# Hybrid decoder layer on one core: strips of the row sums issued together, and the late gathered tiles summed on TensorE

## The chip, the core and the metric

One core of a Trainium2 chip runs the whole layer in one launch. Its engines are TensorE (PE in the profile; its weight loads are PEld), VectorE (DVE), ScalarE (ACT), GpSimd (POOL) and SyncE (SP), each with its own instruction queue, and 16 DMA engines that they share. The metric is the device time of one launch in microseconds; the times are medians over several runs on one chip, and a profile is one execution. Lower is better.

## The reference

One decoder layer on 1024 tokens of 1024 features, in float32. The first half is a mixture of mLSTM heads and dilated attention with an output projection; the second half, where the change lies, is a retrieval of single-neuron experts:

```python
def peer(h, w_query, sub_keys1, sub_keys2, expert_u, expert_v):
    ...
    v1, i1 = lax.top_k(s1, PEER_TOPK)
    v2, i2 = lax.top_k(s2, PEER_TOPK)
    cand = (v1[..., :, None] + v2[..., None, :]).reshape(T, PEER_HEADS, PEER_TOPK * PEER_TOPK)
    vc, ic = lax.top_k(cand, PEER_TOPK)
    ...
    idx = (e1 * N_KEYS + e2).reshape(T, PEER_HEADS * PEER_TOPK)
    gate = jax.nn.softmax(vc, axis=-1).reshape(T, PEER_HEADS * PEER_TOPK)

    def block(args):
        xb, ib, gb = args
        u = expert_u[ib]
        pre = jnp.einsum('td,tkd->tk', xb, u).astype(jnp.float32)
        a = jax.nn.gelu(pre, approximate=False) * gb
        return jnp.einsum('tk,tkd->td', a, expert_v[ib])
```

Each token picks 8 heads x 16 = 128 of 16384 experts; the dot products of its row with 128 rows of `expert_u` give 128 coefficients, and the sum of 128 rows of `expert_v` by these coefficients is added to the token's row `x2`.

## The kernel before

The 1024 tokens are eight tiles of 128, in three groups: tiles 0 and 1, tiles 2 to 5, tiles 6 and 7 (`GROUPS`). Each group passes the projections, attention and mLSTM, the output projection and the queries (`queries`, with `top16` on DVE), and then `pick` makes expert numbers and gates.

The experts are computed in two ways. Group 1 (tiles 2 to 5) is dense: `spread_gates` writes a full table of gates (16384 experts x 512 tokens) through TensorE (L737), ACT and POOL, and `dense_experts` multiplies the tokens with all of `expert_u` (tile pu) and the coefficients with all of `expert_v` (tile pv). Each of these products is three full-width float32r matmuls (L153 to L155) from a high and a low half of both operands; ACT makes the high halves of the tables (L756, L788), DVE the low ones (L758, L790), with two buffers each.

Groups 0 and 2 (tiles 0, 1, 6, 7) are gathered. `experts_in` (U) fetches for each of the 128 picks one row of `expert_u` per token by an indirect DMA issued from POOL (`gather`, L801, 512 KB, five buffers `gt`), and DVE forms the dot product (L813). The sum over `expert_v` (V) has two forms:

- `experts_out`, for the tiles that are not in `ON_PE` (6 and 7): one gather for each pick, and one DVE instruction that multiplies the rows by the coefficient of each token and adds them up (L855).
- `experts_out_pe`, for the tiles in `ON_PE` (0 and 1): here a gather fetches the 128 rows of one token, so the picks lie on the partitions and TensorE sums over them. The coefficients are transposed first (L825), and `pick` has transposed the indices (L700 to L704, tile idxt). The loop runs over two blocks of 64 tokens and 32 steps. A step takes a pair of tokens, 32 apart: DVE builds their weights (L836, tile wv, four buffers), 128 x 32 each, of which one column holds the token's coefficients and the others are zero. Two tokens times two halves of 512 features are four matmuls (L843), each with a 128 x 32 weight and a strip of 32 partitions of the accumulator `po` as target: strips 0 and 2 (q = 0, 2) read the first row buffer of the pair, strips 1 and 3 the second.

The order of the V and U steps is written out at the end: U0 U1 V0 V1 U6 V6 U7 V7. They are traced after all the other work, `dense_experts` too, but the program is ordered by a scheduler that simulates the engines: an instruction takes the first place on its engine at which its operands are ready in the simulation, the earlier in the trace first; within `tc.high_priority()` a matmul goes ahead of whatever else is ready. The order on each engine is then fixed, and on the chip each engine works through it in that order, waiting for semaphores. So the gathered work of tiles 0 and 1 lies beside the attention, the queries and the spreading of group 2 and 1, and that of tiles 6 and 7 beside the dense experts.

Of the kernel before, what the change touches and what calls it, by code (L numbers as in the profile page):

```python
# [11 lines left out]
F32 = mybir.dt.float32  # L12
F32R = mybir.dt.float32r
I32 = mybir.dt.int32
# [6 lines left out]
P = 128  # L21
# [3 lines left out]
NT = T // P  # L25
GROUPS = ((0, 2), (2, 4), (6, 2))
DENSE = 1
ON_PE = (0, 1)
HT = 2
HW = HT * P  # L30
EG = 8
# [3 lines left out]
AH = 8  # L35
# [8 lines left out]
def hybrid_layer(ctx, tc, x, g1, w_in, w_if, conv_w, conv_b, wq, wk, if_b, mh_g, skip, qn_g, kn_g,  # L44
                 rel_bias, onehot, w_out, g2, w_query, keys, expert_u, expert_ut, expert_v, out, dbg=None):
    nc = tc.nc
# [4 lines left out]
    sp = ctx.enter_context(tc.tile_pool(name="sparse", bufs=1))  # L51
# [144 lines left out]
    IDX, IDXT, GATE = {}, {}, {}  # L196
# [442 lines left out]
    def pick(rt, g, t, gr, h0=0, h1=AH):  # L639

        dense = g == DENSE
        H = h1 - h0
        ix = INDS[t][:, :, h0:h1]
        vc, ic = (a[:, h0:h1] for a in BEST[t])

        sh = rt.tile([P, H, 16], U32, name="sh")
        nc.vector.tensor_scalar(sh, ic, 4, 7, op0=ALU.logical_shift_right, op1=ALU.bitwise_xor)
        nc.vector.tensor_scalar(ic, ic, 16, 31, op0=ALU.bitwise_or, op1=ALU.bitwise_and)
        nc.vector.tensor_scalar(ic, ic, 2, None, op0=ALU.logical_shift_left)
        ab = rt.tile([P, 2, H, 16], U32, name="abi")  # L650
        nc.vector.tensor_tensor(ab[:, 0], ic, sh, op=ALU.logical_shift_right)
        nc.vector.tensor_tensor(sh, ab[:, 0], sh, op=ALU.logical_shift_left)
        nc.vector.tensor_tensor(ic, ic, sh, op=ALU.bitwise_xor)
        nc.vector.tensor_scalar(ab[:, 1], ic, 2, 15, op0=ALU.logical_shift_right, op1=ALU.bitwise_and)
        abf = rt.tile([P, 2, H, 16], BF16, name="abf")
        nc.vector.tensor_copy(abf, ab)
        ixf = rt.tile([P, 2, H, 16], BF16, name="ixf")
        nc.vector.tensor_copy(ixf, ix)
        if h0 == 0:
            EF[t] = rt.tile([P, 3, AH, 16], F32, name="ef", bufs=1 if dense else 2)  # L660
            if not dense:
                GATE[t] = sp.tile([P, AH, 16], F32, name="gate", bufs=4)
                IDX[t] = sp.tile([P, P], I32, name="idx", bufs=4)
        ef = EF[t][:, :, h0:h1]
        full = [P, H, 16, 16]
        for s in range(2):
            of = rt.tile(full, BF16, name="of")
            nc.scalar.copy(of, ixf[:, s, :, :, None].to_broadcast(full))
            one = rt.tile(full, BF16, name="one")
            nc.vector.tensor_tensor(one, abf[:, s, :, None, :].to_broadcast(full),  # L670
                                    rank16[:, None].to_broadcast(full), op=ALU.is_equal)
            nc.vector.tensor_tensor(one, one, of, op=ALU.mult)
            for n in (8, 4, 2):
                nc.vector.tensor_tensor(one[:, :, 0:n], one[:, :, 0:n], one[:, :, n:2 * n], op=ALU.add)
            nc.vector.tensor_tensor(ef[:, s], one[:, :, 0], one[:, :, 1], op=ALU.add)
        if not dense:
            e1, e2 = (ef[:, k].rearrange("p h k -> p (h k)") for k in range(2))
            nc.vector.scalar_tensor_tensor(IDX[t][:, h0 * 16:h1 * 16], e1, 128.0, e2, op0=ALU.mult, op1=ALU.add)
        ex = ef[:, 2]
        nc.vector.tensor_tensor(ex, vc, vc[:, :, 0:1].to_broadcast([P, H, 16]), op=ALU.subtract)  # L680
        nc.scalar.activation(ex, ex, AF.Exp)
        sm = rt.tile([P, H], F32, name="smx")
        nc.vector.tensor_reduce(sm, ex, AX.X, ALU.add)
        nc.vector.reciprocal(sm, sm)
        if dense:
            nc.vector.tensor_tensor(ex, ex, sm[:, :, None].to_broadcast([P, H, 16]), op=ALU.mult)
            pe = pst.tile([P, 3, P], F32, name="pe", tag="tp")
            for s in range(3):
                nc.tensor.transpose(pe[:, s], ef[:, s].rearrange("p h k -> p (h k)"), ident)
            ids = gr.tile([P, 2, P], BF16, name="ids", bufs=GROUPS[DENSE][1])  # L690
            nc.scalar.copy(ids, pe[:, 0:2])
            gate = gr.tile([P, P], F32, name="grow", bufs=GROUPS[DENSE][1])
            nc.scalar.copy(gate, pe[:, 2])
            ROWS[t] = ids, gate
        else:
            nc.vector.tensor_tensor(GATE[t][:, h0:h1], ex, sm[:, :, None].to_broadcast([P, H, 16]), op=ALU.mult)
            if t in ON_PE and h1 == AH:
                pe = pst.tile([P, 2, P], F32, name="pei", tag="tp")
                for k in range(2):
                    nc.tensor.transpose(pe[:, k], EF[t][:, k].rearrange("p h k -> p (h k)"), ident)  # L700
                eT = rt.tile([P, P], F32, name="eT")
                nc.scalar.copy(eT, pe[:, 1])
                IDXT[t] = sp.tile([P, P], I32, name="idxt", bufs=len(ON_PE))
                nc.vector.scalar_tensor_tensor(IDXT[t], pe[:, 0], 128.0, eT, op0=ALU.mult, op1=ALU.add)  # L704

    EF = {}
# [92 lines left out]
    def gather(table, idx, j):  # L799
        gt = sp.tile([P, D], F32, name="gt", bufs=5)  # L800
        nc.gpsimd.indirect_dma_start(out=gt, out_offset=None, in_=table,  # L801
                                     in_offset=bass.IndirectOffsetOnAxis(ap=idx[:, j:j + 1], axis=0))
        return gt
# [16 lines left out]
    def experts_out_pe(t):  # L820


        pa = pvs.tile([P, P], F32, name="pat", tag="v")
        with tc.high_priority():
            nc.tensor.transpose(pa, COEF[t], ident)  # L825
        aT = sp.tile([P, 2, 2, 32], F32, name="aT", bufs=1)
        nc.scalar.copy(aT.rearrange("p b j c -> p (b j c)"), pa)
        for b in range(2):
            rows = slice(b * 64, (b + 1) * 64)
            x2 = sp.tile([P, 512], F32, name="x2v", tag="acc", bufs=1)  # L830
            for half in range(2):
                nc.sync.dma_start(x2[half * 64:(half + 1) * 64], x2_d[t][rows, half * 512:(half + 1) * 512])
            po = pvs.tile([P, 512], F32, name="pov", tag="v")
            for c in range(32):
                w = sp.tile([P, 2, 32], F32, name="wv", bufs=4)
                nc.vector.scalar_tensor_tensor(w, iota32[:, None, :].to_broadcast([P, 2, 32]), float(c),  # L836
                                               aT[:, b, :, c:c + 1].to_broadcast([P, 2, 32]),
                                               op0=ALU.is_equal, op1=ALU.mult)
                gts = [gather(expert_v, IDXT[t], b * 64 + j * 32 + c) for j in range(2)]
                with tc.high_priority():  # L840
                    for q in range(4):
                        half, j = divmod(q, 2)
                        nc.tensor.matmul(po[q * 32:(q + 1) * 32], w[:, j], gts[j][:, half * 512:(half + 1) * 512],  # L843
                                         start=c == 0, stop=c == 31)
            nc.vector.tensor_tensor(x2, x2, po, op=ALU.add)
            for half in range(2):
                nc.sync.dma_start(out[t * P + b * 64:t * P + (b + 1) * 64, half * 512:(half + 1) * 512],
                                  x2[half * 64:(half + 1) * 64])
# [37 lines left out]
    for t in range(2):  # L886
        pick(pt_.tiles, 0, t, cl.tiles)
# [24 lines left out]
    for t in range(2, 6):  # L912
        pick(pt_.tiles, 1, t, cl.tiles)
# [16 lines left out]
    for t in range(6, 8):  # L930
        pick(pt_.tiles, 2, t, cl.tiles)
# [10 lines left out]
    for step in "U0 U1 V0 V1 U6 V6 U7 V7".split():  # L942
        t = int(step[1])
        if step[0] == "U":
            experts_in(t)
        else:
            (experts_out_pe if t in ON_PE else experts_out)(t)
    pvsx.__exit__(None, None, None)
# [76 lines left out]
```

## Time and profile before

| | |
|---|---|
| median of 3 runs | 3128.51 us (3125.10 to 3129.28) |
| the profiled execution | 3134.09 us, its span 3132.1 us |
| mean granted clock of TensorE | 0.942 of full speed |
| busy, share of the span | TensorE 91%, DVE 75%, POOL 45%, ACT 39% |
| rows of tables gathered by POOL's DMAs | 536.94 MB of 891.51 MB moved |

The span is the time from the first to the last instruction; the execution's own time is the 2 us longer one. Rows of a profile give a line of the kernel (L843), the engine, the operation, the tiles that it writes and reads (`pov<-gt,wv`; pov is `po` of `experts_out_pe`), how often (x) and busy time. A matmul of float32 operands is two records, one of float32r operands a single one. Busy time is the union of the instructions of a group where they overlap; a matmul's recorded duration is longer than the distance at which the next one starts.

### The profile page before, as it was taken

What the parts mean: (1) busy time and instruction counts of PE and PEld (TensorE: products, weight loads), DVE (VectorE), ACT (ScalarE), POOL (GpSimd) and SP (SyncE); (2) the same over time, 40 slices, a digit from 0 to 9 for tenths busy, and PEclk for the clock granted to TensorE, in tenths of its full rate; (3) what the DMA queues carried; (4) which work ended last, traced back from release to release, by engine and by line L of the source; (5) the groups of instructions that cost most, each with busy time, mean ns of one, the idle gap of its engine ahead of it and who ended that gap; (6) DMA issues with size and microseconds to landing.
All of it is one profiled execution on the core that took longest, in us unless ns stands there. A gap on an engine that the chain in (4) does not pass through costs nothing.

```text
span 3132.1 us, 43008 instructions
## 1 busy us (share of the span) xinstructions
PE 2861.5 (91%) x14382; PEld 2172.5 (69%) x14382; DVE 2353.7 (75%) x5610; ACT 1231.5 (39%) x2270; POOL 1421.7 (45%) x1139
## 2 busy tenths in 40 slices
PE   6967857788869999999989999999999999999999
PEld 5857647577756554467756677788887787887777
DVE  4638997679975677757873588888987888898873
ACT  4633422354423223589984222332322222332222
POOL 0100377436753334544553455555654555554530
PEclk9969978687869999999999999999999999999999
DMA  6534699879998777798888799999999999998982
GB/s 199 173 95 152 224 312 327 278 283 314 348 328 281 239 258 257 260 332 276 301 296 282 276 321 329 330 341 336 331 327 323 326 334 330 349 326 315 324 279 74
DMA packets 370898, 891.51 MB, mean 285 GB/s; under 512 B 34119, under 2 KB 135495, under 8 KB 366580
## 3 DMA queue, kind: packets, MB, share of 16 engines
q0 software_dynamic: 147456, 536.94, 48.7%
q1 hardware_dynamic: 209076, 307.78, 29.9%
q10 hardware_dynamic: 14144, 44.05, 3.7%
q8 instruction: 113, 1.85, 0.2%
q14 instruction: 109, 0.89, 0.1%
HBM read 831.97 MB, written 61.38 MB: 285 GB/s over the span
## 4 chain that ended last, share of the span: by engine, by line
PE 58%; DMA 13%; issue 10%; DVE 10%; POOL 6%; ACT 3%; SPq 1%; POOLq 0%; DVEq 0%; ACTq 0%
PE pov L843 7%; DMA gg<-gate_d 6%; POOL gt L801 6%; PE accq L192 5%; PE pu L153 5%; PE pu L154 5%; PE pu L155 5%; PE pv L154 5%; PE pv L155 5%; PE pv L153 5%; PE pg L737 3%; DMA gt<-in_expert_u_dram,idx 3%; PE acco L192 3%; DVE gt L813 2%; PE sc L509 2%
## 5 line engine op out<-in xcount | busy, mean ns | idle before, releaser
L801 POOL DMA_INDIRECT gt<-in_expert_u_dram,idx x512 | 673.3, 1315 | 611.9 <-DVE gt L813 356.1
L813 DVE SCALAR_TENSOR_TENSOR gt<-gt,h2s 128x1024 f32<-128x1024 f32 x512 | 618.5, 1220 | 75.8 <-DMA gt<-in_expert_u_dram,idx 72.3
L801 POOL DMA_INDIRECT gt<-in_expert_v_dram,idx x256 | 344.6, 1346 | 303.3 <-DVE acc L855 267.7
L801 POOL DMA_INDIRECT gt<-in_expert_v_dram,idxt x256 | 278.4, 1087 | 372.5 <-PE pov L843 316.2
L154 PE MATMUL pv<-vlo,dah 128*128 128x512 f32 x1024 | 404.0, 395 | 13.8 <-DVE vlo L790 13.7
L155 PE MATMUL pu<-h2th,ulo 128*128 128x512 f32 x1024 | 406.8, 397 | 2.5 <-DVE ulo L758 2.5
L153 PE MATMUL pu<-h2th,uhi 128*128 128x512 f32 x1024 | 407.6, 398 | 0.8 <-ACT da L763 0.8
L154 PE MATMUL pu<-h2tl,uhi 128*128 128x512 f32 x1024 | 406.7, 397 | 0.0
L155 PE MATMUL pv<-vhi,dal 128*128 128x512 f32 x1024 | 402.2, 393 | 0.0
L855 DVE SCALAR_TENSOR_TENSOR acc<-gt,act,acc 128x1024 f32<-128x1024 f32 x256 | 327.9, 1281 | 13.2 <-DMA gt<-in_expert_v_dram,idx 10.8
L788 ACT CAST vhi<-vr 128x512 fp32r<-128x512 f32 x256 | 157.5, 620 | 450.5 <-PE pv L155 426.3
L153 PE MATMUL pv<-vhi,dah 128*128 128x512 f32 x1024 | 321.9, 394 | 7.0 <-ACT vhi L788 7.0
L168 ACT CAST wh<-wr 128x512 fp32r<-128x512 f32 x291 | 178.4, 619 | 289.4 <-PE accq L192 67.8
L843 PE MATMUL pov<-gt,wv 128*32 128x512 f32 x1024 | 262.3, 612 | 4.2 <-DMA gt<-in_expert_v_dram,idxt 3.8
L170 DVE TENSOR_TENSOR wl<-wr,wh 128x512 fp32r<-128x512 f32 x291 | 202.1, 699 | 79.1 <-ACT wh L168 71.3
L154 PEld LDWEIGHTS pv<-vlo,dah 128*128 128x128 f32 x1024 | 193.6, 189 | 65.4 <-DVE vlo L790 18.7
L790 DVE TENSOR_TENSOR vlo<-vr,vhi 128x512 fp32r<-128x512 f32 x256 | 175.4, 687 | 81.0 <-ACT vhi L788 80.7
L756 ACT CAST uhi<-ur 128x1024 fp32r<-128x1024 f32 x128 | 134.5, 1051 | 257.8 <-PE pu L154 257.2
L153 PEld LDWEIGHTS pv<-vhi,dah 128*128 128x128 f32 x1024 | 192.7, 189 | 56.1 <-ACT vhi L788 10.0
L153 PEld LDWEIGHTS pu<-h2th,uhi 128*128 128x128 f32 x1024 | 193.2, 189 | 54.4 <-issue 6.7
L155 PEld LDWEIGHTS pu<-h2th,ulo 128*128 128x128 f32 x1024 | 193.1, 189 | 50.0 <-DVE ulo L758 3.0
L154 PEld LDWEIGHTS pu<-h2tl,uhi 128*128 128x128 f32 x1024 | 193.3, 189 | 47.6 <-issue 2.5
(280 smaller groups left out, 5747.2 us busy)
## 6 DMA issues: line engine op xcount, KB each, us to landing
ur<-in_expert_ut_dram SPq DMA_DIRECT2D x128, 512.0 KB
vr<-in_expert_v_dram SPq DMA_DIRECT2D x256, 256.0 KB
wr<-in_w_in_dram SPq DMA_DIRECT2D x144, 256.0 KB
gate_d<-gs ACTq DMA_DIRECT2D x32, 1024.0 KB
gg<-gate_d SPq DMA_DIRECT2D x16, 2048.0 KB
wr<-in_w_query_dram SPq DMA_DIRECT2D x96, 256.0 KB
wr<-in_w_out_dram SPq DMA_DIRECT2D x48, 256.0 KB
gt<-in_expert_u_dram,idx POOLq DMA_INDIRECT x512
```

The source lines that it names most:

```text
L153: nc.tensor.matmul(ps, lh, rh, start=first, stop=False)
L154: nc.tensor.matmul(ps, lh, rl, start=False, stop=False)
L155: nc.tensor.matmul(ps, ll, rh, start=False, stop=last)
L168: nc.scalar.copy(wh, wr)
L170: nc.vector.tensor_tensor(wl, wr, wh.bitcast(F32), op=ALU.subtract)
L192: nc.tensor.matmul(o, l, r, start=k == 0 and c == 0 and j == 0, stop=k == KD - 1 and j == 2, skip_group_check=True)
L788: nc.scalar.copy(vh, vr)
L790: nc.vector.tensor_tensor(vl, vr, vh.bitcast(F32), op=ALU.subtract)
L801: nc.gpsimd.indirect_dma_start(out=gt, out_offset=None, in_=table, in_offset=bass.IndirectOffsetOnAxis(ap=idx[:, j:j + 1], axis=0))
L813: nc.vector.scalar_tensor_tensor(gt, gt, 1.0, h2, op0=ALU.mult, op1=ALU.mult, accum_out=pr[:, j:j + 1])
L843: nc.tensor.matmul(po[q * 32:(q + 1) * 32], w[:, j], gts[j][:, half * 512:(half + 1) * 512], start=c == 0, stop=c == 31)
L855: nc.vector.scalar_tensor_tensor(acc, gt, COEF[t][:, j:j + 1], acc, op0=ALU.mult, op1=ALU.add)
```

## The change

Tiles 6 and 7 join the tiles that sum on TensorE. Their `experts_out` goes, and with it the last use of L855. The four matmuls of a pair are traced in the order of strips 1, 3, 0, 2 in place of 0, 1, 2, 3, and the second to fourth are pinned behind the one before in TensorE's order: the first waits for the second row of the pair. The buffers for indices and for gates go from four to two, those for transposed indices are three instead of two. `gather` and its five buffers and the order of the U and V steps stay.

```diff
-ON_PE = (0, 1)
+ON_PE = (0, 1, 6, 7)
...
-                GATE[t] = sp.tile([P, AH, 16], F32, name="gate", bufs=4)
-                IDX[t] = sp.tile([P, P], I32, name="idx", bufs=4)
+                GATE[t] = sp.tile([P, AH, 16], F32, name="gate", bufs=2)
+                IDX[t] = sp.tile([P, P], I32, name="idx", bufs=2)
...
-                IDXT[t] = sp.tile([P, P], I32, name="idxt", bufs=len(ON_PE))
+                IDXT[t] = sp.tile([P, P], I32, name="idxt", bufs=3)
...
                 with tc.high_priority():
-                    for q in range(4):
+
+                    for k, q in enumerate((1, 3, 0, 2)):
                         half, j = divmod(q, 2)
-                        nc.tensor.matmul(po[q * 32:(q + 1) * 32], w[:, j], gts[j][:, half * 512:(half + 1) * 512],
-                                         start=c == 0, stop=c == 31)
+                        m = nc.tensor.matmul(po[q * 32:(q + 1) * 32], w[:, j],
+                                             gts[j][:, half * 512:(half + 1) * 512], start=c == 0, stop=c == 31)
+                        if k:
+                            tc.keep_in_program_order(m)
```

`keep_in_program_order` gives an instruction an edge to the instruction traced just before it on its engine, for the order alone, without a wait.

## Rows read from the trace of the kernel before

**Rows 1.** Busy time by stretch: us, PE PEld DVE ACT POOL busy, granted clock, DMA, GB/s

```profile
1000.00:1300.00 300.00, 298.30 (x1383) 149.38 (x1377) 211.05 (x1181) 89.22 (x167) 118.48 (x116) 0.99 0.75 248
1300.00:1640.00 340.00, 318.91 (x2045) 218.67 (x2037) 251.29 (x885) 299.34 (x588) 176.96 (x159) 0.98 0.84 298
1640.00:1790.00 150.00, 150.00 (x660) 95.08 (x659) 59.14 (x96) 54.11 (x87) 51.17 (x45) 1.00 0.81 275
1790.00:3030.00 1240.00, 1219.27 (x5231) 985.93 (x5231) 1055.06 (x1408) 363.08 (x547) 670.60 (x499) 0.99 0.94 329
3030.00:3132.00 102.00, 94.96 (x415) 77.44 (x413) 42.82 (x58) 24.29 (x38) 1.93 (x2) 0.98 0.31 104
```

**Rows 2.** The same stretches, line L843 alone: PE and PEld busy (records)

```profile
900.00:1000.00 100.00, 13.15 (x56) 1.89 (x56) 0.94 0.86 297
1000.00:1300.00 300.00, 116.80 (x462) 16.11 (x456) 0.99 0.75 248
1300.00:1640.00 340.00, 97.61 (x386) 13.33 (x378) 0.98 0.84 298
1640.00:1790.00 150.00, 34.72 (x134) 4.76 (x134) 1.00 0.81 275
```

**Rows 3.** Groups of instructions by line and form, whole span

```profile
L855 DVE SCALAR_TENSOR_TENSOR acc<-gt,act,acc 128x1024 f32<-128x1024 f32 x256 | 327.9, 1281 | 13.2 <-DMA gt<-in_expert_v_dram,idx 10.8
...
L843 PE MATMUL pov<-gt,wv 128*32 128x512 f32 x1024 | 262.3, 612 | 4.2 <-DMA gt<-in_expert_v_dram,idxt 3.8 <-DVE wv L836 0.2
...
L836 DVE SCALAR_TENSOR_TENSOR wv<-iota,aT 128x64 f32<-128x64 f32 x128 | 30.7, 242 | 108.6 <-PE pov L843 106.5 <-issue 1.4
```

**Rows 4.** Timeline of PE among the dense matmuls: start us, us, engine, line

```profile
1686.75 0.40 PE L154 MATMUL pu<-h2tl,uhi 128*128 128x512 f32 x1
1686.99 0.40 PE L155 MATMUL pu<-h2th,ulo 128*128 128x512 f32 x1
1687.31 1.06 PE L843 MATMUL pov<-gt,wv 128*32 128x512 f32 x6
1688.30 0.50 PE L153 MATMUL pu<-h2th,uhi 128*128 128x512 f32 x1
1688.64 0.40 PE L154 MATMUL pu<-h2tl,uhi 128*128 128x512 f32 x1
1688.88 0.39 PE L155 MATMUL pu<-h2th,ulo 128*128 128x512 f32 x1
1689.19 1.04 PE L843 MATMUL pov<-gt,wv 128*32 128x512 f32 x2
1690.17 0.50 PE L153 MATMUL pu<-h2th,uhi 128*128 128x512 f32 x1
1690.51 0.40 PE L154 MATMUL pu<-h2tl,uhi 128*128 128x512 f32 x1
```

**Rows 5.** Timeline of PE where the four strips follow one another directly

```profile
1278.36 1.07 PE L843 MATMUL pov<-gt,wv 128*32 128x512 f32 x8
1279.36 1.10 PE L530 MATMUL po<-vp,pb 128*128 128x64 f32 x8
```

**Rows 6.** Groups of PE by line, 1790 to 3030 us: idle before them, releaser

```profile
L154 PE MATMUL pv<-vlo,dah 128*128 128x512 f32 x872 | 344.4, 395 | 13.8 <-DVE vlo L790 13.7
...
L153 PE MATMUL pv<-vhi,dah 128*128 128x512 f32 x869 | 275.4, 394 | 7.0 <-ACT vhi L788 7.0
```

**Rows 7.** Who waited for whom, 1000 to 1790 us: us, times, longest

```profile
DVE wv L836 <- PE pov L843: 95.5, 68, 7.2
```

**Rows 8.** The transposes: ns min/median/max, first and last start in us

```profile
L825 PE MATMUL pat<-ident,act x2: 293/357/421, 900.0 to 1301.4; 128*128 128x128 f32 x2
...
L700 PE MATMUL pei<-ident,ef x4: 270/272/328, 344.2 to 374.5; 128*128 128x128 f32 x4
```

**Rows 9.** Timeline of POOL: last gather of tile 1, first of tile 6, last of tile 7

```profile
1763.65 0.94 POOL L801 DMA_INDIRECT gt<-in_expert_v_dram,idxt  x1 [4.13 <-PE pov L843]
1764.89 1.33 POOL L801 DMA_INDIRECT gt<-in_expert_u_dram,idx  x1 [0.30 <-issue]
...
3032.12 1.87 POOL L801 DMA_INDIRECT gt<-in_expert_v_dram,idx  x1 [2.06 <-DVE acc L855]
```

## The prediction

> **What bounds the kernel now.** I first cut the span into stretches by what runs in them and asked for each engine's busy time in each [rows 1]. From 1000 us to the end TensorE is the engine that is nearly always busy: 298 of 300, 319 of 340, 150 of 150, 1219 of 1240 and 95 of 102 us, at a granted clock of 0.98 to 1.00, that is at 2.4 GHz almost throughout. In the dense experts (1640 us to the end) nothing else is as full: DVE 1055 of 1240 us, DMA 0.94. Only 1300 to 1640 has a second full engine, ACT with 299 of 340 us: the spreading of the gates. So a microsecond of work added to or taken from TensorE counts nearly in full, except in that stretch.
>
> Then I looked where TensorE does the sums that the change touches [rows 2]: the matmuls of tiles 0 and 1 occupy it for 13 + 117 + 98 + 35 = 262 us, all before 1790, in 1038 records. A matmul is two records (1024 for 512 matmuls [rows 3]; a record cut by a window is counted in both), so a pair of gathered rows (four strips) is eight records, and tiles 0 and 1 have 128 pairs. Tiles 6 and 7 do the same sums on DVE: 256 instructions of 1281 ns, 328 us [rows 3], beside a TensorE that is full.
>
> Third, the order inside a pair [rows 4]: six records start together and take 0.99 us, and two records stand alone for 0.98 us with full-width matmuls around them. One strip is issued apart, when the first row of the pair has landed, and three together when the second has. Going through the whole timeline I find the four strips apart in this way in 121 of the 128 pairs; in the other 7 they follow one another directly, and the eight records take 1.07 us, no longer than six [rows 5].
>
> **The change, part by part.**
>
> *Strips together (tiles 0 and 1).* What one visit to the strips costs is read from when the full-width matmuls start [rows 4]. From 1686.99 to 1688.64 two of them and the three strips start: 1.65 us, of which the two would take 2 x 0.235, so the visit costs 1.18 us. The single strip: 1688.88 to 1690.51 is 1.63, so 1.16 us. The strips themselves are 0.98; the other 0.2 is that the full-width matmul before and the one after each take 0.33 instead of 0.235. One visit in place of two takes 1.16 us off each of 121 pairs, 140 us of TensorE time.
>
> The Trainium skill (TensorEngine Tiling (Array Packing), Key Properties) says that a change of tiling mode drains TensorE; it gives no price. It speaks against the change, as 128 visits are added between full-width matmuls; by strips alone the visits to come would sum to 128 x 0.98 = 125 us, with what the rows show on both sides to 151. The trace agrees with the rule, with 0.1 us on each side.
>
> How much of the 140 us reaches the end I take by stretch. 900 to 1300: 65 pairs, about 61 of them apart, 71 us; TensorE is full there, but the stretch mixes attention with the queries and DVE has 211 of 300 us too, so I count 57 (bounds 40 and 71). 1300 to 1640: 48 pairs, about 45 apart, 52 us; ACT has 299 us of work in these 340, so not more than 41 can come off even with ACT never idle, and I count 25 (bounds 0 and 41). 1640 to 1790: 17 pairs, 20 us, in full, as TensorE has no idle time there. Sum 102 us (bounds 60 and 132).
>
> *Tiles 6 and 7 on TensorE.* 128 pairs, one visit each, among the dense matmuls: 128 x 1.18 = 151 us added where TensorE is full (bounds 125, by the strips alone, and 151). Beside it two transposes of indices for each of the two tiles in the picking and one of the coefficients for each in the sums, six in all, at 0.27 to 0.42 us [rows 8]: 2 us. The ACT copies and the index instructions on DVE that follow them hide behind TensorE's other work. DVE loses 328 us and gains 128 builds of weights of 0.24 us [rows 3], 31 us. That does not shorten what TensorE has to do; it can only take idle time from it. In 1790 to 3030 TensorE idles 13.8 us for the low halves that DVE makes and 7.0 for ACT's high halves [rows 6]; a DVE that is 61% instead of 85% busy may give back half, 10 us (bounds 0 and 21).
>
> A wait is added on DVE: the build of a pair's weights waits until TensorE has used an older one (four buffers). In 1000 to 1790 DVE stood 95.5 us for that [rows 7], and the dense low halves are queued behind it. From 1640 to 1790 dense work and these waits run together, and TensorE idles for nothing [rows 1], so I cost it at 0 (bounds 0 and 10); the cover is that DVE is then busy 59 of 150 us.
>
> *POOL and the DMA queues.* The same gathers are issued, of the same bytes. Each buffer is now held until its pair is summed, no longer one row by itself; what that makes of the pace is the first rival. TensorE itself, whose order is fixed, may come to a pair before its rows are there, with everything dense queued behind it: it waited 3.8 us in all for 128 pairs so far, and DVE 10.8 for the 256 rows of the late tiles with DMA at 0.94 [rows 3]. I take 0 (bounds 0 and 11), as the pairs of 1640 to 1790 cost no idle time. The result of a late tile goes through four loads and four stores of 128 KB instead of one each of 512 KB on SP, the same bytes: nothing.
>
> *Two index and gate buffers, three of transposed indices.* Tile 6 takes over buffers of tile 0, whose rows were last read by about 900 us, when its coefficients are transposed [rows 8]; the third transposed buffer's successor, for tile 7, needs tile 0's sums finished, which is so at 1301 [rows 8], and the late tiles are picked after the gates are spread. No wait, 0 (bounds 0 and 5, if the picking of tile 7 were reordered ahead).
>
> **Sum.** 151 + 2 - 102 - 10 = +41 us. Against the profiled execution (span 3132.1, its own time 3134.1) that is 3175. That execution stands 5.6 us above the median of the runs shown, 3128.5, so I forecast 3170, 1.3% slower. With 60 to 132 us saved, 125 to 151 added and 0 to 10 given back by DVE it ranges from 3113 to 3222; with visits at 1.18 us and 90 to 120 us saved it is 3150 to 3180.
>
> **Rivals.**
>
> *The gathers outlast the dense work (slower still).* Now the gathers of the late tiles run from 1765 to 3032 [rows 9], 512 in 1267 us or 2.47 us each, and 100 us of dense work are left behind them. On TensorE a pair took 5.2 us in 1000 to 1300 (58 pairs) and 7.8 from 1640 to some 1772 (17 pairs) [rows 2, 9]. If tile 1 ends 102 us earlier, at 1662, the 256 first-table gathers take 634 us and the last gather has to be issued by 3165, there are 869 us for 128 pairs, 6.8 us each: from there on this rival decides. At 7.8 it is 128 us too long at the slow pace, some 16 pairs; left alone with TensorE and DMA idle they should run at the 4 to 5 us of the fast stretch or below, 70 us, less 19 of TensorE work that leaves the dense part: about 3220. At 7.2, the mean of tile 1 (1301 to 1764 us for 64 pairs [rows 8, 9]), some 3195. For it speaks that the slow pace is the one among dense matmuls; against it that the start of the dense work, with its first loads, is in those 17 pairs.
>
> *The whole saving arrives (no change, or faster).* Place: 900 to 1640. If everything closes up behind TensorE there, 132 us come off (with ACT never idle), and a DVE freed of 297 us lets all 21 us of idle time go: 151 + 2 - 132 - 21 = 0, or 3128; with visits at the strips' 0.98 alone, -26, or 3102. With visits at 1.18 us it decides from 147 us of early and late savings together (then the time is within 0.2% of before, about what a measurement of this kernel can tell) and needs 160 to be faster. For it: TensorE is at 298 of 300 us. Against it: ACT's 299 of 340.
>
> *The strips do not run together.* The third strip in the new order reads the first row, whose landing is a wait of its own; if that wait keeps the strips apart, nothing is saved early and the late tiles pay two visits for a pair, 128 x 2.34 = 300 us: some 3420. Against it stand the 7 pairs that ran in 1.07 us [rows 5]. The same page of the Trainium skill, in the same section, says that different tiles can load and multiply in parallel; the trace agrees, with those 1.07 us for four strips.
>
> **How the numbers follow.** The forecast 0.46, the gathers that outlast the dense work 0.30, the whole saving 0.20 (0.09 faster, 0.11 no change), strips apart 0.04. Slower is 0.80 together. The range goes from 3122, which leaves out most of the faster cases, to 3225, which takes in the tail of gathers and leaves out the strips apart: about 0.15 outside.
>
> **What would show it.** Right: in tiles 0 and 1 eight records start within 0.1 us and last 1.07, and the matmuls' line has 2048 records and some 270 us busy; TensorE busy from 1640 to the end as now, but that stretch longer by 130 to 150 us; the dense work starting 60 to 130 us earlier; DVE at six tenths in the dense part; the last gather of tile 7 before the last dense matmul. Wrong: TensorE idle for gathers among the dense matmuls, gathers after the last dense matmul (first rival), or 1300 to 1640 shrunk by more than 40 us (second). The forecast falls if a visit among dense matmuls costs much less than 1.18 us, or if TensorE's idle time falls by more than the 21 us that I can see.

## The result and the profile after

The change makes the kernel slower: 3238.4 us (median of four runs, 3222.4 to 3253.0) against 3128.9, ratio 1.034 with a 95% interval of 1.0303 to 1.0377. The forecast, 3170 us, had the sign, but the time lies above its range, 3122 to 3225 us. The profiled execution has a span of 3230.7 us, 98.6 more than before. Its page, with busy time, share of the span and instructions of each engine, and the granted clock in forty slices:

```profile
span 3230.7 us, 44729 instructions
...
PE 2914.4 (90%) x15412; PEld 2188.0 (68%) x15412; DVE 2093.5 (65%) x5489; ACT 1235.9 (38%) x2275; POOL 1308.8 (41%) x1139
...
PEclk9989877787789996999989999999999999999999
```

DVE's busy time fell by 260 us and TensorE's grew by 53 (2861.5 before), and the span grew by more than that. Busy time by stretch shows where (columns as in [rows 1], which the first three rows answer to):

```profile
1000.00:1300.00 300.00, 285.08 (x1532) 169.71 (x1532) 228.01 (x1232) 100.22 (x189) 136.33 (x133) 0.89 0.83 282
1300.00:1640.00 340.00, 296.85 (x2111) 230.76 (x2110) 253.27 (x859) 306.02 (x601) 169.68 (x158) 0.97 0.85 303
1640.00:1790.00 150.00, 134.37 (x600) 105.83 (x599) 107.81 (x170) 50.21 (x81) 65.42 (x54) 0.94 0.96 326
...
2100.00:2200.00 100.00, 97.54 (x480) 61.56 (x479) 33.77 (x60) 22.07 (x32) 40.15 (x41) 1.00 0.91 308
...
3000.00:3100.00 100.00, 100.00 (x435) 81.40 (x434) 40.98 (x56) 31.13 (x46) 0.00 (x0) 1.00 0.42 122
```

And the strips' line alone, for the same stretches [rows 2]:

```profile
1000.00:1300.00 300.00, 75.33 (x504) 10.37 (x504) 0.89 0.83 282
1300.00:1640.00 340.00, 51.15 (x384) 7.55 (x384) 0.97 0.85 303
1640.00:1790.00 150.00, 4.26 (x32) 0.63 (x32) 0.94 0.96 326
...
2100.00:2200.00 100.00, 21.31 (x160) 3.17 (x160) 1.00 0.91 308
```

Two things are to be read here. Among the dense matmuls (2100 to 2200) the new strips run, 20 pairs in 100 us, in a TensorE that is as full as before. In 1000 to 1640, where the strips together should have freed time, more pairs are done in less busy time (504 records in 75 us; before it was 462 in 117), yet TensorE is now idle for 15 of 300 and 43 of 340 us, where it was for 2 and 21, and its granted clock in the first stretch is 0.89 in place of 0.99. Part of what was freed became idle time and time at half clock.

To put numbers on the stretches I took, in each trace, the starts of the same matmuls: the 385th of 768 records of the output projection (acco; tile 0's sums have begun or are about to), the last of the attention scores (sc), the last of the gate spreading (pg), the 600th of the 6144 records of the two dense products together (d), the last of the second product (pv). Counted from the records, in us:

```
                      acco    sc    pg     d    pv   acco-sc   sc-pg    pg-d  acco-d    d-pv
before                 935  1282  1681  1813  3125       347     398     132     877    1312
the change             936  1266  1655  1768  3223       330     389     113     831    1456
early part alone       948  1265  1653  1767  3066       317     388     113     819    1299
strips apart           944  1306  1707  1833  3421       362     401     126     889    1588
one late tile          952  1266  1649  1761  3140       314     383     112     809    1379
half columns           949  1277  1667  1780  3179       328     390     113     831    1398
tile 0 apart           965  1325  1710  1824  3133       360     385     114     859    1309
tile 1 apart           936  1260  1662  1776  3084       324     402     114     841    1308
six row buffers        950  1386  1748  1866  3155       437     362     118     916    1289
all buffers            928  1262  1650  1762  3216       333     388     112     834    1453
four row buffers       922  1235  1634  1762  3128       312     399     127     839    1366
strips only            939  1249  1639  1763  3073       310     390     124     824    1310
zero strip             946  1310  1686  1801  3110       364     376     115     855    1309
```

The mark d has to count both products, which run interleaved. The first experiment's expectation goes by the first product alone: its 385th record of 3072, an eighth, comes 61 us earlier in the change than before. But 216 records of the second product lie ahead of that record before the change, and only 148 in the change. These 68 matmuls, 16 us at 0.235 us each, have merely moved behind it, and are no saving.

In the change the dense part is 144 us longer (forecast 151 + 2 - 10 = 143) and what lies between acco and d is 46 us shorter (forecast 102): 98 us together.

Where the difference went can be read from TensorE's records in both parts. Idle is the time without a matmul. Lost is an estimate: half of the time in which TensorE is busy at half clock, as the same four strips take 1.07 us at one clock and 1.94 at the other (timeline below). Work is what is left, about the time that the matmuls would take at full clock throughout:

```
acco-d, then d-pv:    time  idle  lost  work     time  idle  lost  work
before                 877    23     8   846     1312    21     8  1283
the change             831    76    43   712     1456    16     5  1435
early part alone       819    74    33   712     1299    14     2  1283
strips apart           889    36    18   834     1588     8     3  1576
one late tile          809    69    27   714     1379    15     5  1359
half columns           831    81    37   713     1398    16     2  1380
tile 0 apart           859    58    25   776     1309    19     7  1283
tile 1 apart           841    46    20   775     1308    21     5  1282
six row buffers        916   145    58   713     1289     7     0  1282
all buffers            834    69    54   711     1453    15     3  1436
four row buffers       839    85    49   705     1366    54    19  1294
strips only            824    74    34   715     1310    19     9  1283
zero strip             855    66    23   766     1309    17     5  1287
```

The two views of acco to d, before and then the change (columns as in [rows 1]), and the longest of TensorE's waits in them, in the same order:

```profile
935.00:1813.00 878.00, 854.92 (x4593) 526.82 (x4593) 585.21 (x2293) 480.19 (x922) 389.35 (x354) 0.99 0.81 278
```

```profile
936.00:1768.00 832.00, 755.77 (x4589) 531.44 (x4588) 601.92 (x2310) 474.33 (x917) 387.64 (x362) 0.94 0.86 300
```

```profile
PE pg L737 <- ACT gs L738: 5.6, 6, 1.9
PE pov L843 <- DMA gt<-in_expert_v_dram,idxt: 3.8, 6, 1.3
```

```profile
PE pov L844 <- DMA gt<-in_expert_v_dram,idxt: 14.7, 8, 5.6
PE pv L153 <- ACT dah L149: 14.0, 1, 14.0
PE pg L737 <- ACT gs L738: 11.6, 12, 2.6
PE accq L192 <- DVE wl L170: 8.2, 9, 2.0
PE pg L737 <- POOL e L732: 7.9, 5, 3.9
```

Between acco and d the work fell by 134 us, but 53 us of idle time and a loss of some 35 us at half clock came in, and 46 us are left. In the dense part the work grew by 152 us, as the forecast had it (153). The experiments take the two parts of the change apart.

### The profile page after: what moved, and what is told of

Read it like the earlier page. It is cut to its first block, busy times and chain, and to the rows that moved or that the text cites. A ratio compares the mean times of both kernels' runs of the same rounds, so it can differ in the third digit from the quotient of the medians.

```text
span 3230.7 us, 44729 instructions
## 1 busy us (share of the span) xinstructions
PE 2914.4 (90%) x15412; PEld 2188.0 (68%) x15412; DVE 2093.5 (65%) x5489; ACT 1235.9 (38%) x2275; POOL 1308.8 (41%) x1139
## 4 chain that ended last, share of the span: by engine, by line
PE 55%; issue 12%; DMA 12%; DVE 9%; POOL 7%; ACT 4%; SPq 0%; POOLq 0%; ACTq 0%; another core or an unknown queue 0%; DVEq 0%
POOL gt L801 7%; PE pov L844 7%; PE pv L154 5%; PE pv L153 4%; PE pv L155 4%; PE pu L154 4%; PE pu L153 4%; PE pu L155 4%; PE accq L192 4%; DMA gt<-in_expert_v_dram,idxt 3%; DMA gt<-in_expert_u_dram,idx 3%; DMA gg<-gate_d 3%; PE acco L192 2%; PE sc L509 2%; PE pg L737 2%
## 5 line engine op out<-in xcount | busy, mean ns | idle before, releaser
L801 POOL DMA_INDIRECT gt<-in_expert_u_dram,idx x512 | 656.1, 1281 | 634.6 <-DVE gt L813 382.8
L801 POOL DMA_INDIRECT gt<-in_expert_v_dram,idxt x512 | 525.4, 1026 | 678.9 <-PE pov L844 558.8
L153 PE MATMUL pv<-vhi,dah 128*128 128x512 f32 x1024 | 329.0, 396 | 17.7 <-ACT dah L149 14.0
L844 PE MATMUL pov<-gt,wv 128*32 128x512 f32 x2048 | 281.4, 623 | 23.2 <-DMA gt<-in_expert_v_dram,idxt 22.9
L758 DVE TENSOR_TENSOR ulo<-ur,uhi 128x1024 fp32r<-128x1024 f32 x128 | 156.9, 1225 | 157.9 <-ACT uhi L756 146.8
L155 PEld LDWEIGHTS pv<-vhi,dal 128*128 128x128 f32 x1024 | 193.3, 189 | 51.6 <-issue 10.9
```

What stands on the lines that cost most here:

```text
L153: nc.tensor.matmul(ps, lh, rh, start=first, stop=False)
L155: nc.tensor.matmul(ps, ll, rh, start=False, stop=last)
L758: nc.vector.tensor_tensor(ul, ur, uh.bitcast(F32), op=ALU.subtract)
L844: m = nc.tensor.matmul(po[q * 32:(q + 1) * 32], w[:, j], gts[j][:, half * 512:(half + 1) * 512], start=c == 0, stop=c == 31)
```

## The experiments

**The early part alone.**

```diff
-ON_PE = (0, 1, 6, 7)
+ON_PE = (0, 1)
```

> The strips together and the fewer buffers, tiles 6 and 7 left on DVE. Theory A (the changed trace: the early saving is only some 60 us, as the dense work is 61 us earlier at one eighth of its first products, and the late tiles cost some 160): 3055 to 3085 us. Rival B (the forecast's early saving of 102 us arrives when the late tiles are not in the way, and the late tiles cost 200): 3020 to 3040 us.

Measured 3070.7 us, ratio to before 0.9812 (0.9779 to 0.9846). Theory A: strips together and the new numbers of index and gate tiles are a gain of 64 us, and the late tiles on TensorE cost 3238 - 3071 = 167 (165 by the two ratios to before). This is also the fastest kernel of the study.

**Strips apart, all four tiles on TensorE.**

```diff
-                    for k, q in enumerate((1, 3, 0, 2)):
+                    for k, q in enumerate(range(4)):
...
-                        if k:
-                            tc.keep_in_program_order(m)
```

> All four gathered tiles on TensorE with the fewer buffers, the strips in the old order and not pinned. Theory A (every visit to the strips among dense matmuls costs 1.18 us, two for a late pair): 3129 + 300 = 3400 to 3450 us. Rival B (a visit mostly fills time that TensorE would wait anyway, and the late tiles cost the waits for their rows): 3250 to 3330 us.

Measured 3429.8 us, 1.0951 (1.0915 to 1.0987). Theory A; TensorE's work in the dense part grew by 1576 - 1283 = 293 us, 2.29 us a pair for two visits, of which 17 came back as less idle time and half clock. The strips together are what makes the late tiles cost half of that.

**Only one late tile.**

```diff
-ON_PE = (0, 1, 6, 7)
+ON_PE = (0, 1, 7)
```

> As the change, but only tile 7 of the late tiles on TensorE. Theory A (each late tile costs the same, 64 visits of some 1.2 us): halfway between the early part alone and the change, 80 us under the change, 3145 to 3170 us. Rival B (the cost lies in the gathers that reach to the end, so the last tile carries it): 3200 to 3240 us.

Measured 3143.1 us, 1.0030 (1.0005 to 1.0054), a little under theory A's interval. The dense part grew by 1379 - 1312 = 67 us and its work by 76, half of 152: the cost goes by pairs, not by the last tile.

**Half the columns for the late tiles.**

```diff
+        cw = 256 if t > 1 else 512
...
-                        m = nc.tensor.matmul(po[q * 32:(q + 1) * 32], w[:, j],
-                                             gts[j][:, half * 512:(half + 1) * 512], start=c == 0, stop=c == 31)
+                        m = nc.tensor.matmul(po[q * 32:(q + 1) * 32, 0:cw], w[:, j],
+                                             gts[j][:, half * 512:half * 512 + cw], start=c == 0, stop=c == 31)
...
-            nc.vector.tensor_tensor(x2, x2, po, op=ALU.add)
+            nc.vector.tensor_tensor(x2[:, 0:cw], x2[:, 0:cw], po[:, 0:cw], op=ALU.add)
```

> As the change, but the strips of tiles 6 and 7 multiply only the first 256 of their 512 columns; the other half of these sums is left out. Theory A (the price is the time that the strips occupy TensorE): 128 visits shorter by 0.45 to 0.49 us, 58 to 63 us, so 3170 to 3185 us. Rival B (the price is the switch between full width and strips, or a wait for rows, at each visit): 3220 to 3240 us.

Measured 3180.1 us, 1.0155 (1.0131 to 1.0179): theory A. The two timelines of TensorE (start, us, engine, line) show one visit of each kernel. First the change:

```profile
2102.26 0.40 PE L153 MATMUL pu<-h2th,uhi 128*128 128x512 f32 x1
2102.50 0.40 PE L154 MATMUL pu<-h2tl,uhi 128*128 128x512 f32 x1
2102.82 1.07 PE L844 MATMUL pov<-gt,wv 128*32 128x512 f32 x8
2103.82 0.50 PE L153 MATMUL pv<-vhi,dah 128*128 128x512 f32 x1
2104.15 0.40 PE L154 MATMUL pv<-vlo,dah 128*128 128x512 f32 x1
```

Then the one with half the columns:

```profile
2042.59 0.40 PE L153 MATMUL pu<-h2th,uhi 128*128 128x512 f32 x1
2042.91 0.64 PE L845 MATMUL pov<-gt,wv 128*32 128x256 f32 x8
2043.48 0.50 PE L154 MATMUL pu<-h2tl,uhi 128*128 128x512 f32 x1
2043.82 0.40 PE L155 MATMUL pu<-h2th,ulo 128*128 128x512 f32 x1
```

From the full-width matmul before a visit to the second one after it there are 1.65 and 1.23 us, of which the two full-width matmuls take 0.46: a visit costs 1.19 us, and 0.77 with half the columns. The difference, 0.42, times 128 is 54 us; measured 58, and 55 in the work of the dense part (1435 and 1380). So the price is the strips' time in TensorE, plus some 0.2 us around each visit that shorter strips do not change.

**Tile 0 or tile 1 apart, in the early part alone.** The order 0 to 3 and no pinning, for one tile (here tile 0; the other kernel has 1 in its place):

```diff
-                    for k, q in enumerate((1, 3, 0, 2)):
+                    for k, q in enumerate((0, 1, 2, 3) if t == 0 else (1, 3, 0, 2)):
...
-                        if k:
+                        if k and t != 0:
```

> The early part alone (3071 us), but tile 0 with its strips in the old order and not pinned. Theory A (in 900 to 1300 us most of what the shorter visits free is given back, as TensorE then waits for rows and its clock falls to 1.2 GHz for some 45 to 60 us more): undoing it costs only 10 to 30 us, 3080 to 3100 us, and the time at half clock in 900 to 1300 falls back under 20 us. Rival B (the forecast's count for 900 to 1300, 57 to 71 us): 3125 to 3142 us.

> The early part alone, but tile 1 in the old order and not pinned. Theory A (tile 1 carries most of the early saving of 64 us, since its visits stand among spread gates and dense matmuls): 3100 to 3125 us. Rival B (ACT's 300 us in 1300 to 1640 swallow what tile 1's visits free, so the saving is tile 0's): 3075 to 3090 us.

Tile 0 apart: 3129.9 us, 0.9989 (0.9966 to 1.0011), no different from before the change. By the letter that is rival B. But 30 us of it lie ahead of tile 0's sums: the mark acco comes at 965 us, in place of 935. In the mLSTM heads just before it TensorE waits 18.3 and 14.1 us for DVE, where the kernel before waits 12.7 for DVE and 9.6 for a load, and it is at half clock for 33 us between 900 and the mark, before 12; this execution also stands 13 us above the median of its kernel. The order of the whole program is computed anew for each kernel, so that time can change where nothing was edited. From acco to d it takes 859 us, before 877, the early part alone 819: undoing tile 0 costs 40, for 64 us of work (776 - 712). Tile 1 apart: 3109.1 us, 0.9926 (0.9900 to 0.9952), in theory A's interval; but its 841 us from acco to d are only 22 more than 819, for 62 us of work, so the reason given there, that tile 1 carries most, is not borne out by this stretch. Both tiles bring a share, and 58 us together in the early part alone, where the forecast counted 102. The expectation that tile 0's saving is mostly given back fell: 24 of 64 us are. Its half clock in 900 to 1300 is 37 us, not under 20, but only 3 of them lie behind the mark.

A part of what was given back shows in TensorE's waits in 900 to 1300 us, who waited for whom: us, times, longest. Before the change, then the change:

```profile
PE pov L843 <- DMA gt<-in_expert_v_dram,idxt: 1.6, 2, 1.3
```

```profile
PE pov L844 <- DMA gt<-in_expert_v_dram,idxt: 14.4, 7, 5.6
```

With tile 0 apart, and with the early part alone:

```profile
PE pov L844 <- DMA gt<-in_expert_v_dram,idxt: 2.2, 2, 1.2
```

```profile
PE pov L844 <- DMA gt<-in_expert_v_dram,idxt: 15.2, 13, 2.4
```

Wherever tile 0's strips go together TensorE stands 13 to 40 us there for rows that have not landed, in nine kernels (that with the zero strip, below, apart); where they are apart, 1.6 to 2.6, in three. One such wait of the change, in the timeline of TensorE:

```profile
1206.11 1.07 PE L844 MATMUL pov<-gt,wv 128*32 128x512 f32 x8
...
1210.00 1.09 PE L509 MATMUL sc<-kp,qp 64*128 64x512 f32 x2 [1.46 <-DVE ic L653]
1211.03 0.70 PE L416 MATMUL pq<-cT,wqk 128*128 128x256 f32 x2
1213.47 1.94 PE L844 MATMUL pov<-gt,wv 128*32 128x512 f32 x8 [1.75 <-DMA gt<-in_expert_v_dram,idxt]
...
1227.19 1.94 PE L844 MATMUL pov<-gt,wv 128*32 128x512 f32 x8
```

TensorE idles 1.46 us for DVE, then 1.75 for rows, and from then on the same four strips take 1.94 us in place of 1.07: the clock has fallen from 2.4 to 1.2 GHz. The stretch 1220 to 1240, first before and then after the change, has granted clocks of 1.00 and 0.51:

```profile
1220.00:1240.00 20.00, 19.72 (x106) 9.63 (x107) 14.67 (x90) 8.04 (x21) 7.54 (x9) 1.00 0.75 264
```

```profile
1220.00:1240.00 20.00, 20.00 (x65) 11.21 (x64) 11.10 (x31) 7.36 (x12) 4.27 (x4) 0.51 0.35 103
```

TensorE is "busy" for the whole 20 us with 65 matmul records in place of 106. Between 900 and 1300 us it is at half clock for 16 us before, 77 in the change and 51 in the early part alone, of which 12, 12 and 24 lie ahead of acco. Between acco and sc it is 17 to 106 us in the ten kernels with tile 0's strips together, and 0 to 7 in the three with them apart.

**Six and four row buffers.** If the rows are late, another buffer should help.

```diff
-        gt = sp.tile([P, D], F32, name="gt", bufs=5)
+        gt = sp.tile([P, D], F32, name="gt", bufs=6)
...
-                IDXT[t] = sp.tile([P, P], I32, name="idxt", bufs=3)
+                IDXT[t] = sp.tile([P, P], I32, name="idxt", bufs=2)
...
-        pr = sp.tile([P, P], F32, name="pr_s", bufs=2)
+        pr = sp.tile([P, P], F32, name="pr_s", bufs=1)
```

> The early part alone with six row buffers in place of five (two transposed index tiles and one product tile pay for it). Theory A (TensorE comes to a pair before its rows are there, and idles and loses its clock by it): the waits for rows shrink from 15 us to under 5, half clock in 900 to 1300 to under 20 us, 3040 to 3060 us. Rival B (the waits lie elsewhere, the order is what the simulation makes of it): 3063 to 3085 us.

Measured 3164.8 us, 1.0096 (1.0076 to 1.0115), 94 us slower than with five: both expectations missed. Half clock in 900 to 1300 is 123 us. The waits there, and its busy time in 1027 to 1300:

```profile
PE pov L844 <- DMA gt<-in_expert_v_dram,idxt: 40.0, 22, 5.4
```

```profile
1027.00:1300.00 273.00, 222.05 (x1159) 108.39 (x1157) 199.68 (x1145) 68.77 (x115) 141.63 (x133) 0.84 0.90 312
```

The order puts both tiles' pairs ahead (they end at 1469 in place of 1662 us), and TensorE, which cannot pass them, waits for their rows with all of the attention queued behind: 51 of 273 us idle, clock 0.84. The smaller numbers of product and transposed index tiles are in this kernel too; the product tile was not timed by itself. From this I expected that fewer buffers would set the pairs apart and help.

```diff
-        gt = sp.tile([P, D], F32, name="gt", bufs=5)
+        gt = sp.tile([P, D], F32, name="gt", bufs=4)
```

> The early part alone (3071 us) with four row buffers in place of five. Theory A (six buffers made the order pack the pairs closer than their rows can land, 40 us of waits for rows and 89 us of half clock between 1027 and 1300; fewer buffers set them apart): waits for rows under 5 us and half clock under 15 us in 900 to 1300, and 3050 to 3090 us. Rival B (the six buffers' loss is another accident of the order, and four starve the gathers): waits as before or more, 3100 to 3160 us.

Measured 3136.8 us, 1.0019 (0.9994 to 1.0043), with 27 us of waits for rows and 85 of half clock in 900 to 1300: theory A fell, and the time is rival B's. Its dense part is 67 us longer too (1366 after 1299). TensorE idles there for 54 us in place of 14, 42 of them waiting for ACT's high halves (vhi); that the late gathers have a buffer less as well may be behind it, but that is not shown. Five is the fastest of the three, and the waits are no simple matter of how far ahead the order puts a pair.

**A zero strip in tile 0.** A fifth matmul with weights of zero, pinned behind the four, gives TensorE work back without changing the sums:

```diff
+                    if t == 0 and c < 31:
+                        tc.keep_in_program_order(nc.tensor.matmul(po[64:96], wz, gts[0][:, 512:1024], start=False, stop=False))
```

> The early part alone (3071 us) with a fifth strip matmul pinned behind the four of tile 0's pairs, on a strip already used, with weights of zero (62 of them, sums unchanged). Theory A (in tile 0's stretch TensorE waits some 15 us for rows and runs some 45 us longer at half clock than before the change; the added work takes the place of these): 3080 to 3110 us, waits for rows under 8 us and half clock under 20 us in 900 to 1300. Rival B (work on TensorE counts in full there, and waits and clock come from elsewhere): 62 x 0.98 = 61 us, 3125 to 3140 us, waits and half clock as in the early part alone.

Measured 3117.1 us, 0.9911 (0.9879 to 0.9944), between the two. The zero strips occupy TensorE for 64 us. From acco to d its work grows by 766 - 712 = 54 us and the time by 855 - 819 = 36. TensorE's groups and waits in 900 to 1300:

```profile
L851 PE MATMUL pov<-gt,wz 128*32 128x512 f32 x124 | 64.1, 599 | 0.0
```

```profile
PE pov L846 <- DMA gt<-in_expert_v_dram,idxt: 7.7, 3, 4.1
```

The waits for rows fall by half and the half clock in 900 to 1300 from 51 to 35 us, less than theory A asked. Of the 54 us of added work 8 take the place of idle time and some 10 of what half clock cost, and 36 arrive: 0.67 of the work. Tile 0's 64 us, when undone above, cost 40, which is 0.63. In both kernels the order is computed anew, too.

**The numbers of buffers.** Two kernels with four index and four gate tiles: the change so (and four transposed index tiles), and the early part alone so (and two).

```diff
-                GATE[t] = sp.tile([P, AH, 16], F32, name="gate", bufs=2)
-                IDX[t] = sp.tile([P, P], I32, name="idx", bufs=2)
+                GATE[t] = sp.tile([P, AH, 16], F32, name="gate", bufs=4)
+                IDX[t] = sp.tile([P, P], I32, name="idx", bufs=4)
```

> The change with four index and four gate tiles and four transposed index tiles, as many as there are tiles. Theory A (the smaller numbers hold nothing up, cost 0): 3222 to 3253 us as the change. Rival B (the picking of tiles 6 and 7 waits for tiles 0 and 1): 3190 to 3215 us.

> The strips together for tiles 0 and 1 and nothing else: four index, four gate and two transposed index tiles as before the change. Theory A (the numbers of buffers are worth nothing by themselves): 3060 to 3085 us, as the early part alone. Rival B (fewer of them hold something up, as the 18 us between the change and its variant with all buffers suggest): 3045 to 3060 us.

Measured 3220.3 us, 1.0264 (1.0243 to 1.0285), and 3082.3 us, 0.9841 (0.9824 to 0.9857). The first is 18 us under the change, between its two expectations; the second is 12 us over the early part alone, where theory A had it, with intervals that overlap. The fewer buffers look worse in the one and better in the other, so I take neither as their effect; that a newly computed order makes differences of 10 to 20 us by itself is likely, but not shown. What the late tiles cost is 167 us by the one pair of kernels and 138 by the other; the work in the dense part differs by 152 and 153.

## Why the prediction was wrong

- *TensorE bounds the kernel, and the late tiles add to it.* Right. The dense part grew by 144 us and TensorE's work in it by 152.
- *A visit costs 1.18 us among dense matmuls.* Right: 1.19 us, and with half the columns, with two visits and with one late tile the dense part changed as that price says. The 0.2 us around a visit are there in the change and with half the columns. That agrees with the drain at a change of tiling mode of which the Trainium skill tells (TensorEngine Tiling (Array Packing), Key Properties).
- *DVE gives back 10 us; TensorE does not wait for rows.* The first is right and the second is not. TensorE's groups from 1790 us to the end of the change:

```profile
L154 PE MATMUL pv<-vlo,dah 128*128 128x512 f32 x940 | 371.4, 395 | 4.3 <-DVE vlo L790 4.3
...
L153 PE MATMUL pv<-vhi,dah 128*128 128x512 f32 x940 | 302.5, 395 | 3.6 <-ACT vhi L788 3.6
L844 PE MATMUL pov<-gt,wv 128*32 128x512 f32 x1024 | 136.8, 608 | 8.3 <-DMA gt<-in_expert_v_dram,idxt 8.2
```

  The idle time behind DVE and ACT fell from 20.8 us [rows 6] to 7.9, 13 us and not 10, but 8.3 us of waits for rows came in; the forecast had taken 0 out of 0 to 11. Half clock cost some 3 us less. That the sum for the dense part, 143, came out at 144 is partly luck: these three nearly cancel.
- *102 of 140 us saved early.* This is the step that failed: 46 arrived in the change, 58 in the early part alone and 53 with the strips only, all under the lower bound of 60; of the kernels with all strips together only that with one late tile reached it, with 68. The work did go: 134 us in the change (of the 128 pairs 123 stood apart by the records, not 121). By stretch, 900 to 1300 was counted at 57, and acco to sc fell by 17 (30 in the early part alone); 1300 to 1640 was counted at 25, and sc to pg fell by 10, with ACT at 306 of 340 us; 1640 to 1790 was counted at 20, and pg to d fell by 19. I took the first stretch's TensorE, at 298 of 300 us and a clock of 0.99, for a bound that stays as it is when work is taken out of it, and gives back 0.8 of that. It did not stay: from acco to d idle time went from 23 to 76 us and the estimated loss at half clock from 8 to 43. The 140 us had been cut to 102 by judgement, 38 us given back, with no term for idle time or half clock that the change itself brings; 88 of 134 were given back. Of the 53 us more of idle time 24 are waits for ACT, 14.0 of them a single wait for the first coefficients (dah) of the second product, 11 are waits for rows, 7 each for DVE and POOL. So the rows, which come hardly sooner for a visit that is shorter, are the smaller part of the idle time. Half clock is most of the loss in the first stretch: some 25 us there, beside 11 of idle time, in the change.
- *The range.* Its upper end, 3222, leaves out the prediction's own bounds for waits for rows (11), for DVE's builds of weights (10) and for the buffers (5); the measured 3238 needs some of these or a saving under 60.
- *The execution against the median.* The forecast took 5.6 us off, as the profiled execution of before stood that far above its median; that of the change stands 5.9 below its own. That is 12 us of the miss of 68; the early saving is 56, the dense part 1.
- *The gathers outlast the dense work* fell. The late pairs ran at 4.6 us each (the 64 of tile 6 from 1999 to 2293 us, those of tile 7 from 2619 to 2914), not 6.8 or slower (the early stretch that I took at 4 to 5 us had run at 5.2), and the last gather was issued 317 us before the last dense product:

```profile
2906.44 1.65 POOL L801 DMA_INDIRECT gt<-in_expert_v_dram,idxt  x1 [2.98 <-PE pov L844]
```

- *The whole saving arrives* fell with the early stretches. *The strips do not run together* fell too: in all 256 pairs the eight records follow one another directly, in 1.07 us among dense matmuls; its price, 3420, came out at 3430 where they were kept apart.

What is not settled is why each wait came in, and how much of it a better order would bring back. The records say where the freed time went, but no experiment takes away idle time or half clock alone: the waits for rows and half clock come together wherever tile 0's strips go together. That the single strips had before filled time in which ACT, DVE and POOL were not ready fits the waits, but is argued and not shown.

## What to carry to other kernels

Before work is moved to an engine that is already full, price one visit from the trace, with what the neighbours lose on both sides, and multiply: half the columns, two visits and one tile of two all followed that product. Time taken off the bounding engine is worth less than its length where other engines and transfers then make it wait and its clock falls: here 43 to 68 us of 131 to 135, in the six kernels with both early tiles' strips together, five row buffers and nothing added. A stretch should be compared between marks with the same work on both sides: a mark on one of two interleaved products put 16 us into the wrong part. Two good-looking edits in one change should be timed apart; the strips together gain 1.6 to 1.9% without the late tiles, which turn that into a loss of 3.4%.

## What was not expected of the hardware

The time of one and the same kernel follows its time at half clock. In 13 executions of the kernel before, on one chip, the mean granted clock went from 0.947 at 3123.3 us to 0.939 at 3144.5; with the time at half clock taken as twice the missing share of the span (331 to 384 us), a straight line through them has 0.36 us per microsecond at half clock. Nine more on that chip gave 0.48, and on two other chips it was 0.29 (13 executions) and 0.17 (9). And an edit that only shortens TensorE's work can lower its clock: with the change TensorE is at half clock for 61 more microseconds in 900 to 1300 us; in the timeline above its clock falls after waits of 1.46 and 1.75 us.
